# Moving searches, gathered rows and branch products between the stages of a transformer block on one Trainium2 core

## The chip, the core and the metric

The kernel runs on one core of one Trainium2 chip. The metric is the device time of one execution in microseconds; shown are the median of three runs and one further execution that was profiled. A core has five engines that work beside each other and wait for each other by semaphores: TensorE (PE in the profile, with its weight loads as PEld), VectorE (DVE), ScalarE (ACT), GpSimd (POOL) and SyncE (SP, which here only issues transfers). Transfers are issued from SP, ACT and POOL. The matrix engine writes to eight banks (PSUM); everything else lies in the core's memory of 128 partitions.

## What is computed

One residual block over 512 frames and 16 meta tokens, width 2048, in float32:

```python
hn = rmsnorm(h, g_mix);  proj = hn @ w_in          # c_q, c_kv, k_rope, q/k/v_sb, gate_a, gate_b
y_a = mla_attention(...)                           # 8 heads, softmax, chunk-causal
y_b = stick_breaking_attention(...)                # 8 heads
h = h + (sig(gate_a) * (y_a @ w_branch_a) + sig(gate_b) * (y_b @ w_branch_b)) @ w_out
xn = rmsnorm(h, g_ffn)                             # PEER: 8 heads, 16384 experts
s = einsum('thcd,hcnd->thcn', xn @ w_q, sub_keys)  # 2 x 128 scores for each head
s1, i1 = top_k(s[:, :, 0], 16); s2, i2 = top_k(s[:, :, 1], 16)
idx, g = best 16 of the 16 x 16 sums, softmax      # "routing"
h = h + sum_k g_k * gelu(u[idx_k] . xn) * v[idx_k]
out = rmsnorm(h, g_final)                          # meta tokens dropped
```

A product in full float32 is made of three products of rounded parts: the helper `mm3` (lines 258 to 261) multiplies the low part of the weight with the high part of the data, high with low, and high with high.

## The kernel before

Everything is laid out transposed: the width lies on the partitions in 16 pieces of 128, the tokens along the free dimension. The stages follow each other in one long Python function, `body`, that unrolls all loops.

**Weights.** Each weight tile of 128 x 1024 goes the same way (`wtile`, lines 232 to 253): SP loads it into a raw tile `wr` (four of them in rotation, `raw_half`, line 230), ACT rounds it into `wh` (L245), DVE, or POOL for some, subtracts to get `wl` (L246). A raw tile is free again when the subtraction has read it. `wh` and `wl` have three tiles each; two more lie in the tail of `hgh`/`hgl` during the expert loop, and one more in a pool of its own in the output stage.

**Mixer.** Projections, stick-breaking attention and gates, then MLA head by head: in each round of `run(...)` the scores of head h+1 (`mla_s`), the projections of head h+2 (`mla_p`) and the output of head h (`mla_y`) take turns. In the last head only `mla_y` is left. After that the stick-breaking output `yb` is split into high and low parts (eight splits, one for each head), and in the branch loop each of 16 blocks m needs one product with `wa` and one with `wb` (24 matrix products of 512 columns each), both multiplied by a gate. Then `w_out`.

**Scores.** For 16 blocks hc (head and half) PE computes the query block with `wq` in 48 products of 512 columns and the scores of the block before it for four token tiles (`scores`). DVE finds the sixteen highest of each score row by `top16`: MAX8, FIND_INDEX8, MATCH_REPLACE8, MAX8, FIND_INDEX8 (L917 to L921), for token tiles 3, 2, 0 and 1 in this order. The 184 last tokens (all of tile 3 and 56 of tile 2) take their experts' rows one by one: for each of 184 slots POOL gathers 128 rows of `u` by an indirect transfer (1 MB, `send`, L1052) and DVE multiplies and sums them (`row_step`, L1065), later the same with `v` (L1073). The routing of tile 3 (`early`) runs beside the score blocks, ten steps after every fourth block. From hc = 5 on each block ends with one row step.

**Expert loop.** For the other 328 tokens all 16384 experts are computed: e = 0 to 127, each e is two halves of 24 products of 328 columns (`u_products`). After each half `beside(hf)` gives DVE and PE other work: a step of the gates (`gating`: for each pair of tokens one DVE comparison L1256, four ACT scalings L1263, four small PE products L1252, and every 16 tokens a store to memory `g_d` from POOL), the row steps that are due (`rows_due`, with the due count interpolated in `PACE`), and steps of the routing of tiles 2, 0 and 1 (`routing`, a generator of `route` with 30 steps for each tile). Routing steps: one for each e below 8, two for each e from 8 to 23, from then on three for every two e. Gating of a tile starts when its routing is done. At e = 120 the first group's gates are read back (`group_in(0)`).

**Output stage.** 32 groups by 8 blocks of `vb`; each block is two column blocks c of 12 products of 328 columns, added into `acc` (L1498, L1500) unless the next group goes on in the same bank. The remaining 168 row steps are spread over these by `PACE_V`. At the end the squares of `acc` are summed over 16 column blocks (`fin_add`, L1420 and L1422), a product with ones gives the sum over partitions (`rstd`, L301), ACT and DVE form the inverse root (L309 to L315), DVE scales all 16 blocks (L1429), SP stores them (L1431). The last 184 columns go first (`fin_out(ND, SEQ)`), the other 328 at the very end (`fin_out(0, ND)`).

**Order.** The order of the instructions on each engine is fixed when the kernel is built, from the order of the text, the dependencies and an estimate of when things are ready; in the trace it is not simply the order of the text (the first product of the branch loop stands among the last head's products, at 964.09 us). `add_manual_dep(..., NOSYNC)` only keeps an instruction behind another in that order. Each engine then works strictly through its own list.

Of the kernel before, what the change touches and what calls it, by code (L numbers as in the profile page):

```python
# [2 lines left out]

# [20 lines left out]
P = 128  # L24
# [8 lines left out]
H = 8  # L33
# [182 lines left out]
def body(tc, nc, a, dbg=None):  # L216
# [12 lines left out]
    def raw_half():  # L229
        return wp.tile([P, 1024], F32, name="wr", tag="wr", bufs=4)  # L230
# [32 lines left out]
    def split(hi, lo, src, eng=None):  # L263
        S.activation(hi, src, AF.Copy)
        (eng or V).tensor_sub(lo, src, hi.bitcast(F32))
# [26 lines left out]
    xn_d = dp.tile([NB, D], F32, name="xn_d")  # L292
    xr_d = dp.tile([2, P, D], F32, name="xr_d")
# [532 lines left out]
    for m in range(KC):  # L826
        acc = []
        for name, yh_, yl_, gi in (("wa", *ys[0], 0), ("wb", *ys[1], 1)):
            gt = sp2.tile([P, SEQ], F32, name="g2", bufs=4)
            SP.dma_start(gt, gates[gi, m])  # L830
            wh, wl = front(name, m)
            ps = ps_tile()
            for k in range(8):
                s = slice(k * P, (k + 1) * P)
                mm3(ps, wh[:, s], wl[:, s], yh_[:, k], yl_[:, k], k == 0, k == 7)
# [187 lines left out]
    PACE = (0, 14, 60, NK - 0.5), (11, 28, 97, NU)  # L1023
# [7 lines left out]
    gs = {"sent": 0, "done": 0, "pool": None, "gated": False, "six": None, "third": False, "x": 1, "rows": None, "vi": None}  # L1031
# [65 lines left out]
    with tc.tile_pool(name="score", bufs=2, side="right") as sp_:  # L1097
# [8 lines left out]
        def scores(hc, qh, ql):  # L1106
# [8 lines left out]
            for ti in (3, 2, 0, 1):  # L1115
# [9 lines left out]
        for hc in range(16):  # L1125
            ps = ps_tile()
            for hf in range(2):
                wh, wl = wq.pop((hc, hf)) if (hc, hf) in wq else front("wq", hc, hf, G if hf else V)
                for k in range(8):
# [25 lines left out]
            split(qh, ql, ps)  # L1155
# [191 lines left out]
    for e in range(NK):  # L1347
# [67 lines left out]
    rf = ap2.tile([P, SEQ], F32, name="rf")  # L1415

    def fin_add(c, t0, t1, first):
        t = slice(t0, t1)
        sq = ssf if first else vp.tile([P, SEQ], F32, name="fsq", bufs=1)
        S.activation(sq[:, t], acc[:, c, t], AF.Square)  # L1420
        if not first:
            V.tensor_add(ssf[:, t], ssf[:, t], sq[:, t])  # L1422

    def fin_out(t0, t1):
        sc = vp.tile([P, D], F32, name="sc", tag="row", bufs=1).rearrange("p (k t) -> p k t", t=SEQ)
        rstd(rf[:, t0:t1], ssf[:, t0:t1], t1 - t0, D, [sc[:, k] for k in range(3)], None)
# [103 lines left out]
```

## Time and profile before

| | |
|---|---|
| median of 3 runs | 3457.99 us (3455.57 to 3458.05) |
| the profiled execution | 3459.31 us, of it the span of the core 3457.6 us |
| granted TensorE clock | 0.995 |
| PE, PEld busy | 99%, 92% of the span |
| DVE, ACT, POOL busy | 74%, 41%, 22% |
| moved by DMA | 919.94 MB, mean 266 GB/s |
| stages, us from the start of the span | mixer to about 965, branch and w_out to 1317, scores to 1519, expert loop to 2488, output stage to the end |

How to read it: a row of the busy-time view gives, for a stretch from A to B, its length and for each engine the busy time and in brackets the number of instructions, then the granted clock, the busy share of the DMA engines and GB/s. A row of the timeline gives start, duration, engine, line, operation, the tiles written and read, their shapes and a count; in square brackets the idle time before it and who ended it. PE's busy time counts overlapping, pipelined products, so that a stretch with PE busy throughout may still hold fewer products than another: the number in brackets is to be read with it.

### The profile page before, as it was taken

The page shows a single profiled execution, that of the slowest core. Times are in us where ns is not written, and L with a number is a line of the kernel's source. Part 1 is how long each engine was busy: PE and PEld are TensorE (multiplying, and loading weights), DVE is VectorE, ACT ScalarE, POOL GpSimd, SP SyncE. Part 2 cuts the span into 40 slices and gives each one's busy share as a digit, 9 for nine tenths or more (in the row PEclk, how much of TensorE's full clock was granted, in tenths as well). Part 3 has the DMA queues.
Part 4 walks back from the last instruction along what each step waited for, and adds up shares of the span by engine and source line. Part 5 has one row for each costly group of instructions (what it writes and reads, how often), then busy time and mean ns, then how long its engine had stood idle before and what let it go on. Part 6 is the DMA issues. An engine that isn't in the chain of part 4 may idle for free.

```text
span 3457.6 us, 53380 instructions
## 1 busy us (share of the span) xinstructions
PE 3420.5 (99%) x21115; PEld 3188.2 (92%) x21115; DVE 2573.5 (74%) x3573; ACT 1427.4 (41%) x2304; POOL 776.1 (22%) x555
## 2 busy tenths in 40 slices
PE   9999999999999999999999999999999999999997
PEld 8988888887888888889999999999999999999997
DVE  5533334445754557999999988887889999999997
ACT  4233333334543223223576776774333333333333
POOL 1000000000001113322333333333213333333320
PEclk9999999999999999999999999999999999999998
DMA  5322323232144345559999999999999999999993
GB/s 171 100 98 100 98 100 100 89 101 74 62 131 143 129 143 181 204 214 367 377 389 407 405 412 412 405 401 398 403 362 375 394 408 400 402 382 399 409 381 116
DMA packets 227141, 919.94 MB, mean 266 GB/s; under 512 B 27806, under 2 KB 53518, under 8 KB 179090
## 3 DMA queue, kind: packets, MB, share of 16 engines
q1 hardware_dynamic: 134660, 466.11, 36.6%
q0 software_dynamic: 60480, 411.68, 30.0%
q10 hardware_dynamic: 31750, 38.75, 3.1%
q8 instruction: 165, 2.70, 0.3%
q14 instruction: 86, 0.70, 0.1%
HBM read 854.57 MB, written 62.91 MB: 265 GB/s over the span
## 4 chain that ended last, share of the span: by engine, by line
PE 81%; DVE 11%; DMA 4%; issue 2%; ACT 1%; SPq 0%; POOL 0%; DVEq 0%; ACTq 0%
PE ps L259 26%; PE ps L260 25%; PE ps L261 25%; DMA wr<-vb 3%; DVE wl L246 3%; DVE xg L1073 1%; DVE row L1065 1%; PE ps L1252 1%; DVE acc L1073 1%; DVE acc L1500 1%; DVE hgl L246 0%; ACT wh L245 0%; DVE hin L1337 0%; DMA row<-u,eo 0%; DVE acc L1429 0%
## 5 line engine op out<-in xcount | busy, mean ns | idle before, releaser
L245 ACT ACTIVATE wh<-wr 128x1024 fp32r<-128x1024 f32 (+1 forms) x654 | 687.8, 1053 | 1402.6 <-PE ps L261 1038.7
L246 DVE TENSOR_TENSOR wl<-wr,wh 128x1024 fp32r<-128x1024 f32 (+1 forms) x639 | 812.0, 1279 | 391.5 <-ACT wh L245 389.3
L259 PE MATMUL ps<-vah,wl 128*128 128x328 f32 x2048 | 643.8, 314 | 7.0 <-DVE wl L246 6.8
L260 PE MATMUL ps<-val,wh 128*128 128x328 f32 x2048 | 642.7, 314 | 0.0
L261 PE MATMUL ps<-vah,wh 128*128 128x328 f32 x2048 | 639.7, 312 | 0.0
L259 PE MATMUL ps<-hgh,wl 128*128 128x328 f32 (+1 forms) x1488 | 490.9, 330 | 2.8 <-DVE wl L246 2.8
L261 PE MATMUL ps<-hgh,wh 128*128 128x328 f32 (+1 forms) x1488 | 486.1, 327 | 0.0
L260 PE MATMUL ps<-hgl,wh 128*128 128x328 f32 (+1 forms) x1488 | 485.8, 326 | 0.0
L259 PE MATMUL ps<-xh,wl 128*128 128x512 f32 (+1 forms) x1376 | 468.1, 340 | 1.5 <-ACT xh L366 1.5
L260 PE MATMUL ps<-xl,wh 128*128 128x512 f32 (+1 forms) x1376 | 465.0, 338 | 0.8 <-DVE xl L367 0.8
L261 PE MATMUL ps<-xh,wh 128*128 128x512 f32 (+1 forms) x1376 | 464.9, 338 | 0.0
L259 PEld LDWEIGHTS ps<-vah,wl 128*128 128x128 f32 x2048 | 386.3, 189 | 9.5 <-DVE wl L246 9.3
L260 PEld LDWEIGHTS ps<-val,wh 128*128 128x128 f32 x2048 | 387.1, 189 | 0.0
L261 PEld LDWEIGHTS ps<-vah,wh 128*128 128x128 f32 x2048 | 386.8, 189 | 0.0
L1052 POOL DMA_INDIRECT row<-v,eo x128 | 215.5, 1684 | 481.4 <-DVE xg L1073 414.4
L1073 DVE SCALAR_TENSOR_TENSOR xg<-row,act,xg 128x2048 f32<-128x2048 f32 x127 | 297.5, 2343 | 1.2 <-DMA row<-v,eo 1.1
L1065 DVE SCALAR_TENSOR_TENSOR row<-row,xg 128x2048 f32<-128x2048 f32 x128 | 292.1, 2282 | 4.8 <-DMA row<-u,eo 4.8
L259 PEld LDWEIGHTS ps<-hgh,wl 128*128 128x128 f32 x1488 | 280.1, 188 | 14.6 <-DVE wl L246 3.4
L261 PEld LDWEIGHTS ps<-hgh,wh 128*128 128x128 f32 x1488 | 280.1, 188 | 11.7 <-issue 0.2
L260 PEld LDWEIGHTS ps<-hgl,wh 128*128 128x128 f32 x1488 | 280.4, 188 | 10.9
L259 PEld LDWEIGHTS ps<-xh,wl 128*128 128x128 f32 x1376 | 258.6, 188 | 30.2 <-ACT xh L366 3.0
L260 PEld LDWEIGHTS ps<-xl,wh 128*128 128x128 f32 x1376 | 259.1, 188 | 29.1 <-DVE xl L367 1.7
(517 smaller groups left out, 6057.6 us busy)
## 6 DMA issues: line engine op xcount, KB each, us to landing
wr<-ut SPq DMA_DIRECT2D x256, 512.0 KB, 9.4
wr<-vb SPq DMA_DIRECT2D x256, 512.0 KB, 8.0
wr<-front SPq DMA_DIRECT2D x238, 512.0 KB, 3.3
g_d<-gb POOLq DMA_DIRECT2D x42, 512.0 KB, 10.9
gin<-g_d SPq DMA_DIRECT2D x32, 672.0 KB, 7.4
h_d<-hb ACTq DMA_DIRECT2D x128, 164.0 KB, 8.3
hin<-h_d SPq DMA_DIRECT2D x32, 656.0 KB, 8.9
gates<-gt ACTq DMA_DIRECT2D x32, 256.0 KB, 2.0
```

Of the source, the lines that this page charges most:

```text
L245: more["last"] = S.activation(hi[:, s], r, AF.Copy)
L246: sub = (eng or V).tensor_sub(lo[:, s], r, hi[:, s].bitcast(F32))
L259: T.matmul(ps, wl, xh, start=start, stop=False)
L260: T.matmul(ps, wh, xl, start=False, stop=False)
L261: T.matmul(ps, wh, xh, start=False, stop=stop)
L1052: G.indirect_dma_start(out=row, out_offset=None, in_=a[src], in_offset=bass.IndirectOffsetOnAxis(ap=eos[part][:, k:k + 1], axis=0))
L1065: ins = V.scalar_tensor_tensor(row, row, 1.0, xs[part], ALU.mult, ALU.mult, accum_out=w)
L1073: ins = V.scalar_tensor_tensor(y, row, w, y, ALU.mult, ALU.add)
L1252: T.matmul(bank[:, o:o + P], ohs[q % 4][:, 1, :, t], wos[:, q % 4, c, :, t], start=c == 1, stop=c == 0)
L1500: mark = V.tensor_add(acc[:, c, :ND], acc[:, c, :ND], ps[:, :ND])
```

## The change

There are seven edits.

1. **Fifth raw weight tile in the output stage.** When the extra weight pool is open, every fifth raw tile comes from it.
2. **Branch products ahead.** In the last two heads of MLA a new generator splits all eight heads of `yb` into tiles that lie where the MLA inputs were, and computes the `wb` products of blocks 0, 1 and 2 into PSUM banks that stay held (`ready`). In the run of head 6 it may take nine steps, in the run of head 7 all the rest. The branch loop then takes these three from `ready`. The eight splits at the start of the branch stage stay, for blocks 3 to 15.
3. **One token tile's searches put off.** `scores` no longer searches tile 1; it stores its scores to memory (`s_d`, one store from the ACT queue for each block). After the routing of tile 0, four loads of four blocks each on the SP queue bring them back, into the tile that the candidates of the routing use, and 16 searches follow as routing steps.
4. **Rows earlier.** From hc = 11 a second row step stands in the middle of each score block, and `PACE` is (16, 38, 101, 200) in place of (11, 28, 97, 200) at e = 0, 14, 60 and 127.5.
5. **Routing steps.** They begin after e = 5 and come at an even rate of 1.5 for each e.
6. **Gating steps.** Every fourth e takes one more.
7. **Output.** The squares of the 328 columns get a second tile; the last column block's square isn't added on DVE, PE adds it in PSUM behind a product with the sum of the other fifteen; the inverse root takes fewer DVE instructions; the stores are in smaller groups.

The core of the diff:

```diff
     def raw_half():
+        if more["pool"] is not None and more["n"] % 5 == 0:
+            return more["pool"].tile([P, 1024], F32, name="wr", tag="wr")
         return wp.tile([P, 1024], F32, name="wr", tag="wr", bufs=4)
...
+    s_d = dp.tile([P, 2 * H, NK], F32, name="s_d")
...
+    AHEAD = 3
+    ready = {}
+    def branch_ahead():
+        bh, bl = ([lp.tile([P, 4, n], F32R, name=x, tag=t)[:, :, :SEQ] for t, n in ((f"cq{p}", SEQ), (f"ck{p}", LEN))]
+                  for x, p in (("ybh", "h"), ("ybl", "l")))
+        for h in range(H):
+            split(bh[h // 4][:, h % 4], bl[h // 4][:, h % 4], yb[:, h])
+            yield
+        for m in range(AHEAD):
+            wh, wl = front("wb", m)
+            ps = ready[m] = ps_tile()
+            for k in range(8):
+                s = slice(k * P, (k + 1) * P)
+                mm3(ps, wh[:, s], wl[:, s], bh[k // 4][:, k % 4], bl[k // 4][:, k % 4], k == 0, k == 7)
+                if k % 2:
+                    yield
...
+        if h == H - 2:
+            ahead = branch_ahead()
+        run(*([mla_s(h + 1)] if h + 1 < H else []), *([mla_p(h + 2)] if h + 2 < H else []), mla_y(h),
+            *([ahead] if h == H - 1 else [islice(ahead, 9)] if h == H - 2 else []))
...
+            if gi and m in ready:
+                ps = ready.pop(m)
+            else:
...
-    PACE = (0, 14, 60, NK - 0.5), (11, 28, 97, NU)
+    PACE = (0, 14, 60, NK - 0.5), (16, 38, 101, NU)
...
-            for ti in (3, 2, 0, 1):
+            S.dma_start(s_d[:, hc], sc[:, 1])
+            for ti in (3, 2, 0):
...
+                if hf and hc > 10:
+                    row_step(more["dve"], 2)
...
             yield from route(ti, 4, rk)
             routed.append(ti)
+            for h0 in range(0, 2 * H if ti == 0 else 0, 4):
+                sc = rk.tile([P, 512], F32, name="sc4", tag="cand", bufs=1).rearrange("p (h n) -> p h n", n=NK)
+                ld = SP.dma_start(sc, s_d[:, h0:h0 + 4])
+                tc.add_manual_dep(ld.ins, more["last"].ins.name, NOSYNC, reason="not before its turn")
+                for _ in range(3):
+                    yield
+                for h in range(4):
+                    top16(v1[:, 1, h0 + h], i1[:, 1, h0 + h], sc[:, h], NK)
+                    yield
...
-            next(gate_steps, None)
+            for _ in range(2 if hf and e % 4 == 0 else 1):
+                next(gate_steps, None)
...
-            for _ in range(hf if e < 8 else 1 if e < 24 or e % 2 else hf):
+            while gs["steps"] < 1.5 * (e + hf / 2 - 5):
+                gs["steps"] += 1
...
+    def fin_last(c):
+        ps = final["ps"] = ps_tile()
+        T.matmul(ps[:, :ND], ones, ssf[:, :ND], start=True, stop=False)
+        sq = vp.tile([P, ND], F32, name="fsq", bufs=2)
+        S.activation(sq, acc[:, c, :ND], AF.Square)
+        T.matmul(ps[:, :ND], ones, sq, start=False, stop=True)
+
+    def fin_end():
...
+        S.activation(t, ps, AF.Ln, scale=1.0 / D, bias=C("eps"))
+        V.tensor_scalar(v, ps, 1.0 / D, EPS, ALU.mult, ALU.add)
+        S.activation(r0, t, AF.Exp, scale=-0.5)
+        V.tensor_mul(v, v, r0)
+        V.scalar_tensor_tensor(v, v, -0.5, r0, ALU.mult, ALU.mult)
+        V.scalar_tensor_tensor(rf, v, 1.5, r0, ALU.add, ALU.mult)
+        for c0, n in ((0, 1), (1, 1), (2, 2), (4, 2), (6, 2), (8, 2), (10, 2), (12, 2), (14, 1), (15, 1)):
```

More of the change, by code (lines that the diff above doesn't have):

```diff
@@ L2 @@
 from contextlib import ExitStack
+from itertools import islice
 import numpy as np
@@ L264, in split @@
         S.activation(hi, src, AF.Copy)
-        (eng or V).tensor_sub(lo, src, hi.bitcast(F32))
+        return (eng or V).tensor_sub(lo, src, hi.bitcast(F32))
     def dump(name, ap):
@@ L830, in body @@
             SP.dma_start(gt, gates[gi, m])
[L831 to L835, printed above, removed]
+            if gi and m in ready:
+                ps = ready.pop(m)
+            else:
+                wh, wl = front(name, m)
+                ps = ps_tile()
+                for k in range(8):
+                    s = slice(k * P, (k + 1) * P)
+                    mm3(ps, wh[:, s], wl[:, s], yh_[:, k], yl_[:, k], k == 0, k == 7)
             sg = S.activation(gt, gt, AF.Sigmoid)
@@ L1030, in body @@
     rcols = [rcol] + [rcolb[:, j:j + 1] for j in range(len(cuts))]
-    gs = {"sent": 0, "done": 0, "pool": None, "gated": False, "six": None, "third": False, "x": 1, "rows": None, "vi": None}
+    gs = {"sent": 0, "done": 0, "pool": None, "gated": False, "six": None, "third": False, "x": 1, "steps": 0, "rows": None, "vi": None}
     rows = {}
@@ L1154, in body @@
                 S.dma_start(xn_d, xgb[:NB])
-            split(qh, ql, ps)
+            more["dve"] = split(qh, ql, ps)
             late.append((hc, qh, ql))
@@ L1414, in body @@
     ssf = ap2.tile([P, SEQ], F32, name="ssf")
-    rf = ap2.tile([P, SEQ], F32, name="rf")
     def fin_add(c, t0, t1, first):
         t = slice(t0, t1)
-        sq = ssf if first else vp.tile([P, SEQ], F32, name="fsq", bufs=1)
-        S.activation(sq[:, t], acc[:, c, t], AF.Square)
+        sq = ssf[:, t] if first else vp.tile([P, ND], F32, name="fsq", bufs=2)[:, :t1 - t0]
+        S.activation(sq, acc[:, c, t], AF.Square)
         if not first:
-            V.tensor_add(ssf[:, t], ssf[:, t], sq[:, t])
+            V.tensor_add(ssf[:, t], ssf[:, t], sq)
     def fin_out(t0, t1):
         sc = vp.tile([P, D], F32, name="sc", tag="row", bufs=1).rearrange("p (k t) -> p k t", t=SEQ)
+        rf = sc[:, 3]
         rstd(rf[:, t0:t1], ssf[:, t0:t1], t1 - t0, D, [sc[:, k] for k in range(3)], None)
@@ L1431, in fin_out @@
             SP.dma_start(a["out"][c0:c0 + n, :, t0:t1].rearrange("k p t -> p k t"), acc[:, c0:c0 + n, t0:t1])
+    final = {}
+    def fin_last(c):
[5 more added lines that the diff above has]
+    def fin_end():
+        sc = vp.tile([P, D], F32, name="sc", tag="row", bufs=1).rearrange("p (k t) -> p k t", t=SEQ)
+        v, r0, t, rf = (sc[:, k, :ND] for k in range(4))
+        ps = final["ps"][:, :ND]
+        S.activation(t, ps, AF.Ln, scale=1.0 / D, bias=C("eps"))
[5 more added lines that the diff above has]
+        for c0, n in ((0, 1), (1, 1), (2, 2), (4, 2), (6, 2), (8, 2), (10, 2), (12, 2), (14, 1), (15, 1)):
+            for c in range(c0, c0 + n):
+                V.scalar_tensor_tensor(acc[:, c, :ND], acc[:, c, :ND], gain("fin")[:, c:c + 1],
+                                       rf, ALU.mult, ALU.mult)
+            SP.dma_start(a["out"][c0:c0 + n, :, :ND].rearrange("k p t -> p k t"), acc[:, c0:c0 + n, :ND])
     banks_of, begun, done = {}, {STAY[0] * 2 + c for c in range(4)}, []
@@ L1504, in body @@
                 if i >= NG - 1 and not stays:
-                    fin_add(c, 0, ND, not done)
+                    if len(done) == KC - 1:
+                        fin_last(c)
+                    else:
+                        fin_add(c, 0, ND, not done)
                     done.append(c)
@@ L1509, in body @@
     assert sorted(done) == list(range(KC))
-    fin_out(0, ND)
+    fin_end()
     fin.close()
```

1 line of the change is left out of this document (removed).

## The prediction

> **What bounds the kernel now.** I read the page first, then who makes PE wait, then the busy times of short stretches to find where PE stands still.
>
> ```profile
> span 3457.6 us, 53380 instructions
> PE 3420.5 (99%) x21115; PEld 3188.2 (92%) x21115; DVE 2573.5 (74%) x3573; ACT 1427.4 (41%) x2304; POOL 776.1 (22%) x555
> PE ps L259 <- DVE wl L246: 9.6, 8, 2.4
> ```
>
> PE is the bound: it idles 37.1 us in all, and the change takes no product away. So only idle PE can be won, and what follows an idle PE. Eight waits for DVE's subtraction (9.6 us) are the only large ones. The stretches (from:to, length, then busy time and instructions of PE, PEld, DVE, ACT, POOL, granted clock, DMA share, GB/s) show where:
>
> ```profile
> 950.00:965.00 15.00, 12.88 (x80) 10.11 (x79) 11.02 (x34) 8.08 (x23) 0.00 (x0) 1.00 0.00 1
> 975.00:980.00 5.00, 5.00 (x24) 4.14 (x23) 3.43 (x3) 1.69 (x2) 1.28 (x1) 1.00 0.49 155
> 1415.00:1540.00 125.00, 124.58 (x646) 106.65 (x646) 122.49 (x454) 32.63 (x42) 29.90 (x19) 1.00 0.56 193
> 1540.00:1545.00 5.00, 2.63 (x16) 2.37 (x15) 5.00 (x25) 2.81 (x4) 2.25 (x2) 0.92 0.41 103
> 1545.00:1550.00 5.00, 5.00 (x27) 5.00 (x27) 4.71 (x8) 1.71 (x3) 0.94 (x1) 0.74 0.96 376
> 1550.00:1582.00 32.00, 32.00 (x215) 31.59 (x214) 31.89 (x79) 14.06 (x17) 8.05 (x6) 1.00 0.97 379
> 1820.00:1825.00 5.00, 3.85 (x26) 3.59 (x25) 2.81 (x6) 1.06 (x1) 0.98 (x1) 1.00 1.02 378
> 2505.00:2510.00 5.00, 4.50 (x30) 4.23 (x29) 5.00 (x5) 1.06 (x1) 1.68 (x1) 1.00 0.97 350
> 2525.00:2530.00 5.00, 3.65 (x24) 3.38 (x23) 5.00 (x5) 2.12 (x2) 1.49 (x2) 1.00 1.01 369
> 2530.00:2535.00 5.00, 4.56 (x20) 4.56 (x21) 5.00 (x6) 0.00 (x0) 0.94 (x1) 0.66 0.96 368
> 2555.00:2560.00 5.00, 3.66 (x24) 3.26 (x23) 5.00 (x5) 1.18 (x2) 2.61 (x2) 1.00 0.78 275
> 2560.00:2565.00 5.00, 3.21 (x21) 2.95 (x20) 5.00 (x6) 1.06 (x1) 0.94 (x1) 0.98 1.04 418
> 2565.00:2570.00 5.00, 5.00 (x25) 5.00 (x25) 5.00 (x5) 0.00 (x0) 0.94 (x1) 0.68 0.98 404
> 2575.00:2580.00 5.00, 5.00 (x36) 5.00 (x35) 2.84 (x4) 2.20 (x3) 0.00 (x0) 1.00 1.01 410
> 2580.00:3380.00 800.00, 798.91 (x5323) 797.90 (x5323) 750.87 (x636) 267.59 (x248) 261.37 (x150) 1.00 0.99 391
> ```
>
> The reader should see five places. At the end of the mixer (950 to 965) PE idles 2.12 us. At the start of the expert loop (1540) it idles 2.37 us, and then the granted clock falls to 0.74 and 27 products fit where an undisturbed 5 us hold 36: 9 x 0.14 = 1.3 us more. At 1820 it idles 1.15 us. In the first 80 us of the output stage the idle times are 0.50 + 1.35 + 0.44 + 1.34 + 1.79 = 5.4 us, and the slow clock after them costs 12 products in 2530 to 2535 (20, where 4.56 us hold 32) and 11 in 2565 to 2570, 23 x 0.14 = 3.2 us: 8.6 us. Afterwards (2580 to 3380) 1.1 us in 800. The last place is the tail, below.
>
> **The end: minus 1.0 us.** After the last product of the output stage a chain runs alone (DVE but for the second row).
>
> ```profile
> 3441.20 0.50 DVE L1422 TENSOR_TENSOR ssf<-ssf,fsq 128x328 f32<-128x328 f32 x1 [0.60 <-ACT fsq L1420]
> 3441.76 1.22 PE L301 MATMUL ps<-ssf,cst 128*128 128x328 f32 x2 [2.32 <-DVE ssf L1422]
> 3443.57 0.50 DVE L310 TENSOR_SCALAR sc<-ps 128x328 f32<-128x328 f32 x1 [1.88 <-ACT sc L309]
> 3444.08 0.50 DVE L312 TENSOR_TENSOR sc<-sc 128x328 f32<-128x328 f32 x1
> 3445.52 0.50 DVE L315 TENSOR_TENSOR rf<-sc 128x328 f32<-128x328 f32 x1
> 3446.05 7.62 DVE L1429 SCALAR_TENSOR_TENSOR acc<-acc,gn,rf 128x328 f32<-128x328 f32 x16
> ```
>
> The addition at 3441.20 goes (0.50), as PE starts on the square itself. From 3444.08 to 3446.05 four instructions make the root, 1.97 us; three of 0.50 make 1.5, another 0.47 saved. The new product with the sum of fifteen blocks is ready one block earlier and hidden by the last addition and square; uncovered it costs half of 1.22. The 16 scalings stay, and the stores behind them keep their last two pieces, so smaller groups in front I take at nothing (between 0 and -1). Together -1.0, from -2 to -0.3.
>
> **Branch products ahead: minus 2 us.** 72 products at 5 us for 24 make 15 us of work that waits for nothing but the splits, beside an idle time of 2.12 us. The price is on DVE and ACT, where the eight splits are made a second time:
>
> ```profile
> 966.22 4.90 DVE L265 TENSOR_TENSOR yl_b<-yb,yh_b 128x512 fp32r<-128x512 f32 x8
> ```
>
> 4.9 us more on DVE, which is busy 11.0 of the 15 us: 15.9 in 15. That delays the last head's output by about 1 us, but PE has the 15 us of products to do meanwhile. The three weights come earlier on SP, ACT and DVE and are not loaded twice. The second set of splits gets its memory only when the products ahead are done; `wa` of blocks 0 to 3 (four times 5 us) covers these 5 us. Three of eight banks are held, none is lacking. If PE reaches the first product before the splits, the 4.9 us show: -2.1 to +5. I take -2, as the work at hand is seven times the hole.
>
> **Score blocks and start of the expert loop: plus 3 us.** DVE decides: it is busy 122.5 of 125 us from 1415, and 31.9 of 32 after the hole. Prices:
>
> ```profile
> L1065 DVE SCALAR_TENSOR_TENSOR row<-row,xg 128x2048 f32<-128x2048 f32 x128 | 292.1, 2282 | 4.8 <-DMA row<-u,eo 4.8
> L919 DVE MATCH_REPLACE8 wk<-lists,sc 128x128 f32<-128x128 f32 x64 | 17.5, 274 | 0.0
> L921 DVE FIND_INDEX8 lists<-lists,wk 128x8 uint32<-128x128 f32 x64 | 18.1, 283 | 0.0
> L987 DVE TENSOR_TENSOR oh<-oh,step 128x1024 f16<-128x1024 f16 x2 | 1.4, 688 | 0.0
> 1572.78 1.19 DVE L246 TENSOR_TENSOR wl<-wr,wh 128x1024 fp32r<-128x1024 f32 x1
> 1574.18 0.31 PE L259 MATMUL ps<-hgh,wl 128*128 128x328 f32 x1
> L1052 POOL DMA_INDIRECT row<-u,eo x128 | 169.2, 1322 | 468.5 <-DVE row L1065 284.0 <-DVE lists L917 45.2 <-DVE tv L920 35.6
> ```
>
> A row step is 2.28 us, a search five instructions of 0.27 to 0.28, 1.4 us. The pair of DVE and PE shows how little is in hand near e = 8 (by the count of products it begins near 1582): the weight is ready at 1573.97, the product that needs it starts at 1574.18. So the sum goes from 1415, where DVE has no more slack (block 8), to e = 8. Rows: `PACE` and the five extra steps make 29 instead of 21, 8 x 2.28 = +18.2. Searches: nine blocks lose one, 9 x 1.4 = -12.6. Routing: by the step counts four or five of tile 2's steps instead of eight; those not yet due are the unpacking and two one-hot builds of 0.69, some -2.7. Sum +2.9 us, and each of them moves PE, since DVE is full on both sides. Bounds: if the first score blocks from 8 on now leave DVE idle, the searches of three are saved for nothing: +7. If the hole at 1540 closes, because routing has not begun there, and the overload finds routing steps to put off: -3.7. I take +3.
>
> Gathers move with the rows: two in a block of 12.6 us (1317 to 1519 for 16); POOL is busy 29.9 of 125 us there and takes 1.3 us for one; queued behind it is its own weight subtraction. The 16 stores of `sc` stand in ACT's queue; ACT is busy 32.6 of 125. Nothing for both.
>
> **Later routing: minus 1.15 us.** After e = 14 the rows come at 63 for 46 e instead of 69, so DVE gets slack where it was full, and the 16 searches (22 us) fall between e = 48 and 64. The hole at 1820, one late DVE subtraction, should be covered. The four loads on SP wait for the candidate tile; weight loads stand behind them and the cast of the weights waits for those. In cover is about one half (3.6 us); uncovered +2 for each of four. By counted steps gating ends at e = 116.5 instead of 110.5. The first group's gates are read at e = 120; 3.5 x 7.1 us (48 products at 215 in 32 us) = 25 us are enough for a store of
>
> ```profile
> g_d<-gb POOLq DMA_DIRECT2D x42, 512.0 KB, 10.9
> ```
>
> **Fifth raw tile: minus 6 us.** What leads to the holes at 2525 (DVE, ACT):
>
> ```profile
> 2503.20 2.35 DVE L1073 SCALAR_TENSOR_TENSOR acc<-row,actb,acc 128x2048 f32<-128x2048 f32 x1
> 2505.47 4.62 DVE L246 TENSOR_TENSOR wl<-wr,wh 128x1024 fp32r<-128x1024 f32 x4
> 2512.10 1.49 DVE L1337 TENSOR_TENSOR hin<-hin,gin 128x1280 f32<-128x1280 f32 x1 [2.01 <-issue]
> 2517.05 1.22 DVE L246 TENSOR_TENSOR wl<-wr,wh 128x1024 fp32r<-128x1024 f32 x1 [3.36 <-ACT wh L245]
> 2515.96 1.06 ACT L245 ACTIVATE wh<-wr 128x1024 fp32r<-128x1024 f32 x1 [8.62 <-DMA wr<-vb]
> wr<-vb SPq DMA_DIRECT2D x256, 512.0 KB, 8.0
> ACT wh L245 <- DMA wr<-vb: 200.0, 62, 10.2
> ```
>
> DVE is behind, does four subtractions in a row, frees four raw tiles at once; the loads take 8 us, ACT waits 8.6, DVE stands idle 5.4 us, and then has rows and weights at once and makes PE wait at 2525. The same again at 2555. One more raw tile is loaded during the burst, so that one subtraction (1.2 us) falls into DVE's idle time. Each of the two groups (about 2 us and the slow clock, then 3.1 us and the slow clock) loses at least 1.2, probably with it the fall of the clock. Of 8.6 us I take two thirds, -6. Bounds: -9.5 with the waits after 2580; +7 below.
>
> **Sum:** -1.0 - 2.0 + 3 - 1.15 - 6 = -7.15 us. Profiled execution: 3459.31, of it 1.7 outside the span, so 3452.2; the median shown lies 1.3 lower, at 3457.99: forecast 3450.8 us. About 0.2%, 6.9 us, is what a measurement of this kernel can tell from no change; the forecast is just beyond.
>
> **Rivals.** (1) All holes close: -2 at the end, -2.1, -3.7, -1.15, -8.6: 3440.4. For it: every edit aims at a place where PE idles, and DVE's load later falls. Against: eight more rows in a stretch where DVE is full. (2) The holes of the output stage only move, since rows, not loads, put DVE behind (a row of 2.35 us stands right ahead of the four subtractions): the V term is 0 and the time 3456.8; the change then does not do there what it says. (3) The start of the expert loop takes it: +7 and a second fall of the clock, 1.3, in place of +3: 3456.1. (4) Slower: the fifth load joins the burst. DMA is at 0.99 from 2580 on and at 0.97 to 1.04 in most rows of the holes; five loads of 512 KB take 5/4 of the 8.6 us, 2.2 us more at each of three bursts, which a DVE that is busy 750.9 of 800 us does not make up: +6.5, and two falls of the clock more, 3: 3466. It decides once a burst frees all five. [...]
>
> **How the numbers follow.** Forecast 0.45 (own range 3446 to 3455), (1) 0.22, (2) 0.15, (3) 0.08, (4) 0.10. Faster by over 0.2% (below 3451.1): half of the forecast and (1), 0.45; slower (above 3464.9): most of (4), 0.08; else 0.47. The range leaves out (4) and the lower third of (1): 3440 to 3461.
>
> **What would show it.** Right: in 950 to 965 PE busy throughout; a chain end of 1 us less; in the first 80 us of the output stage at most half of the idle time and one or no fall of the clock; leads near zero and a hole of 2 to 6 us between e = 0 and 14; PE full around e = 40. Wrong: a hole at the splits; ACT waiting longer for `wr<-vb` than 200 us in all; no hole in the expert loop, then rows cost less than reckoned.

## The result and the profile after

The changed kernel takes 3477.04 us (median of 6 runs, 3469.95 to 3480.45); the kernel before took 3457.24 us in the 6 runs beside it (3454.25 to 3462.2). The ratio is 1.0058, with a 95% interval from 1.0046 to 1.0070: slower by about 20 us, where 7 us of gain were forecast. The profiled execution took 3478.51 us, its span is 3476.7 us. Of the medians below one leaves out an execution: a_turn_four_rows_back once took 5570.83 us at a granted clock of 0.562.

First the page of the kernel after, then three rows of its waits (who waited and for whom: us in total, times, longest):

```profile
span 3476.7 us, 53463 instructions
...
PE 3430.7 (99%) x21117; PEld 3197.5 (92%) x21117; DVE 2578.0 (74%) x3579; ACT 1422.1 (41%) x2312; POOL 755.8 (22%) x555
```
```profile
ACT wh L248 <- DMA wr<-vb: 31.6, 11, 8.3
...
DVE lists L945 <- DMA sc<-s_d: 18.3, 2, 9.2
...
PE ps L262 <- DVE wl L249: 13.4, 7, 4.5
```

PE stands 46.0 us where it stood 37.1, and is "busy" 10.2 us longer with practically the same products (two records more), mainly in slow clock: before the last 40 us the clock records of the trace stand at half speed for 47.8 us in all, those of the kernel before for 20.5. The second row is new: twice DVE stood still, 18.3 us in all, for the scores that come back from memory. The busy times of short stretches of the kernel after (columns as in the prediction) show the same places as before, and as new ones one in the last score block (1500) and two around 1870 and 1950:

```profile
945.00:965.00 20.00, 19.16 (x110) 15.03 (x110) 16.23 (x48) 10.80 (x31) 0.00 (x0) 1.00 0.14 47
1500.00:1505.00 5.00, 3.80 (x23) 3.21 (x22) 5.00 (x18) 0.00 (x0) 1.27 (x1) 1.00 0.47 187
1505.00:1510.00 5.00, 5.00 (x16) 3.95 (x15) 4.93 (x9) 2.33 (x4) 0.95 (x1) 0.66 0.71 230
1545.00:1550.00 5.00, 1.71 (x9) 1.72 (x10) 5.00 (x10) 3.01 (x4) 0.99 (x1) 0.93 0.94 347
1550.00:1555.00 5.00, 5.00 (x26) 5.00 (x26) 5.00 (x13) 0.07 (x1) 1.08 (x2) 0.72 0.98 392
1820.00:1825.00 5.00, 5.00 (x40) 4.89 (x39) 5.00 (x7) 3.65 (x10) 1.72 (x1) 1.00 1.04 353
1865.00:1870.00 5.00, 3.21 (x22) 2.94 (x20) 1.51 (x10) 1.62 (x3) 0.00 (x0) 1.00 0.48 194
1870.00:1875.00 5.00, 2.51 (x9) 2.51 (x10) 5.00 (x16) 0.83 (x1) 0.09 (x1) 0.52 0.39 136
1945.00:1950.00 5.00, 3.85 (x29) 3.58 (x25) 1.03 (x8) 0.00 (x0) 0.00 (x0) 1.00 0.87 353
1950.00:1955.00 5.00, 1.11 (x4) 1.11 (x5) 4.97 (x21) 0.80 (x3) 0.00 (x0) 0.71 0.08 12
2515.00:2520.00 5.00, 1.25 (x9) 0.98 (x7) 0.53 (x1) 1.62 (x2) 0.00 (x0) 0.87 0.60 248
2520.00:2525.00 5.00, 4.25 (x15) 4.25 (x16) 5.00 (x5) 1.33 (x2) 0.94 (x1) 0.50 0.35 107
2530.00:2535.00 5.00, 2.54 (x11) 2.27 (x10) 5.00 (x5) 1.06 (x1) 3.28 (x2) 0.74 0.92 319
```

At the end of the mixer 0.84 us of idle PE are left of 2.12. The start of the expert loop is worse (1500, 1545). The hole at 1820 is closed. But at 1865 to 1875 and 1945 to 1955 PE stands 4.3 and 5.0 us and then runs slowly, and in the first row of each DVE is busy for only 1.51 and 1.03 us of 5: no engine is overloaded there, something is being waited for. The holes at the start of the output stage have changed their place, but they are not gone.

**A ledger of stages.** The trace holds every product `ps<-..,wl` or `ps<-..,hgl` of the expert loop (2048, sixteen for each e) and of the output stage (2048, 64 for each group), so number 16e starts block e, and the difference of two such starts is exactly what a stage took. Lengths of the stages in the profiled executions, in us, all so worked out (the columns add up to the span but for rounding):

| kernel | to scores | scores to e = 8 | e 8 to 44 | e 44 to 64 | e 64 to output | groups 0 to 3 | rest | span |
|---|---|---|---|---|---|---|---|---|
| before | 1317.2 | 264.4 | 272.3 | 153.8 | 480.3 | 125.0 | 844.5 | 3457.6 |
| after | 1314.6 | 268.6 | 267.0 | 169.5 | 485.5 | 126.3 | 845.1 | 3476.7 |
| a_no_loads | 1316.5 | 268.9 | 270.6 | 157.6 | 482.5 | 123.9 | 842.9 | 3463.0 |
| a_in_turn | 1314.7 | 268.4 | 266.8 | 154.4 | 485.5 | 127.8 | 838.0 | 3455.5 |
| a_act_loads | 1314.2 | 267.6 | 267.0 | 161.6 | 485.0 | 128.9 | 841.1 | 3465.5 |
| a_four_in_scores | 1316.7 | 279.1 | 270.6 | 152.9 | 483.2 | 122.6 | 842.5 | 3467.6 |
| a_turn_four | 1314.2 | 268.5 | 270.8 | 152.8 | 482.7 | 124.1 | 843.5 | 3456.5 |
| a_turn_four_rows_back | 1316.5 | 259.1 | 269.2 | 155.0 | 488.7 | 121.9 | 847.7 | 3458.1 |
| a_turn_late | 1316.7 | 267.2 | 266.6 | 155.3 | 487.5 | 117.8 | 838.0 | 3449.0 |
| best_mid | 1314.6 | 262.0 | 273.6 | 153.1 | 486.5 | 119.4 | 841.0 | 3450.3 |
| b_ahead_out | 1315.2 | 264.3 | 272.5 | 154.9 | 480.3 | 121.5 | 845.1 | 3453.8 |
| b_ahead_out_fifth | 1315.1 | 264.4 | 273.4 | 153.9 | 480.3 | 126.8 | 843.2 | 3457.0 |
| b_fifth_late | 1316.1 | 264.2 | 272.1 | 153.9 | 480.3 | 119.0 | 843.8 | 3449.3 |
| best_two_rows | 1314.7 | 265.0 | 270.9 | 156.0 | 480.6 | 118.4 | 841.6 | 3447.4 |

So the 19.1 us between the two spans are -2.6 + 4.2 - 5.3 + 15.7 + 5.2 + 1.3 + 0.6. Most of it lies between e = 44 and 64. For example, the rows from which that column comes, of the kernel before and of the kernel after:

```profile
1853.91 0.31 PE L259 MATMUL ps<-hgh,wl 128*128 128x328 f32 x1
...
2007.76 0.32 PE L259 MATMUL ps<-hgh,wl 128*128 128x328 f32 x1
```
```profile
1850.22 0.40 PE L262 MATMUL ps<-hgh,wl 128*128 128x328 f32 x1
...
2019.73 0.32 PE L262 MATMUL ps<-hgh,wl 128*128 128x328 f32 x1
```

One profiled execution of each kernel stands behind a row; stages without any edit between two kernels differ by up to some 2 us (the first column of those with branch products ahead goes from 1314.2 to 1316.7), and up to some 7 us in the last one, where clock falls come and go (before the last 40 us the clock stands at half speed for 6.8 us of it in the kernel before, for 17.1 in the kernel after). The profiled execution of a_in_turn is the fastest of its ten (3457.28 us). The medians further down are therefore read beside the ledger; those of runs made at different times have kernels before of 3456.86 to 3459.04 us beside them, so that a difference between two of them is better taken from their ratios.

**What happens at 1856.** From the timelines of SP, ACT, DVE and PE of the kernel after, in this order:

```profile
1856.00 0.42 SPq L1327 DMA_DIRECT2D sc<-s_d  x1
...
1861.91 1.06 ACT L248 ACTIVATE wh<-wr 128x1024 fp32r<-128x1024 f32 x1 [2.67 <-DMA wr<-ut]
...
1865.71 1.06 ACT L248 ACTIVATE hgh<-wr 128x1024 fp32r<-128x1024 f32 x1 [2.74 <-DMA wr<-ut]
...
1858.25 1.16 DVE L249 TENSOR_TENSOR hgl<-wr,hgh 128x1024 fp32r<-128x1024 f32 x1
...
1868.49 0.49 DVE L945 MAX8 lists<-sc 128x8 f32<-128x128 f32 x2 [9.08 <-DMA sc<-s_d]
...
1871.22 1.21 DVE L249 TENSOR_TENSOR wl<-wr,wh 128x1024 fp32r<-128x1024 f32 x1
...
1872.49 0.64 PE L262 MATMUL ps<-hgh,wl 128*128 128x328 f32 x1 [4.28 <-DVE wl L249]
```

The load of four blocks' scores is issued at 1856.00. DVE has finished its last subtraction at 1859.41, and next in its fixed order stands the first search. It waits 9.08 us, until 12.5 us after the issue. Meanwhile ACT has rounded two weights (1862.97, 1866.77) whose subtractions stand behind the search. The first of them is done at 1872.43, and PE, out of weights, starts at 1872.49. The third of the four does the same (SP, DVE, PE):

```profile
1936.07 0.43 SPq L1327 DMA_DIRECT2D sc<-s_d  x1
...
1948.97 0.29 DVE L945 MAX8 lists<-sc 128x8 f32<-128x128 f32 x1 [9.23 <-DMA sc<-s_d]
...
1953.89 0.64 PE L262 MATMUL ps<-hgh,hgl 128*128 128x328 f32 x1 [5.04 <-DVE hgl L249]
```

The change keeps the load behind a weight's rounding and lets three routing steps pass in the text; but nothing kept the searches behind those steps, so they moved up in DVE's order to right behind the load.

### The profile page after: what moved, and what is told of

The parts are those of the page before. It is cut to its first block, busy times and chain, and to the rows that moved or that the text cites. A ratio compares the mean times of both kernels' runs of the same rounds, so it can differ in the third digit from the quotient of the medians.

```text
span 3476.7 us, 53463 instructions
## 1 busy us (share of the span) xinstructions
PE 3430.7 (99%) x21117; PEld 3197.5 (92%) x21117; DVE 2578.0 (74%) x3579; ACT 1422.1 (41%) x2312; POOL 755.8 (22%) x555
## 4 chain that ended last, share of the span: by engine, by line
PE 70%; DVE 13%; DMA 9%; issue 4%; ACT 2%; POOL 1%; SPq 0%; DVEq 0%; ACTq 0%; POOLq 0%
PE ps L262 22%; PE ps L263 22%; PE ps L264 22%; DMA wr<-ut 6%; DVE row L1093 4%; DVE wl L249 2%; DVE hgl L249 1%; DMA sc<-s_d 1%; ACT wos L1294 1%; POOL row L1080 1%; ACT wh L248 1%; DMA wr<-vb 1%; DMA g_d<-gb 0%; DVE more_oh L1287 0%; DMA row<-u,eob 0%
## 5 line engine op out<-in xcount | busy, mean ns | idle before, releaser
L1080 POOL DMA_INDIRECT row<-v,eo x128 | 203.0, 1586 | 481.3 <-DVE xg L1101 430.2
```

The source lines that it names most:

```text
L1080: G.indirect_dma_start(out=row, out_offset=None, in_=a[src], in_offset=bass.IndirectOffsetOnAxis(ap=eos[part][:, k:k + 1], axis=0))
```

## Experiments

Theory A is the paragraph above: DVE stands in order in front of the data. Rivals for the loss between e = 44 and 64 were B (weight loads are late, queued on SP behind the four loads: the prediction's own view) and C (22 us of searches are too much). For the output stage they were D (the holes only move), E (the prediction: the fifth raw tile gains) and F (one load more in flight lengthens the others); G (the first load into the fifth tile comes late) was added from the order of the loads on SP. H says that DVE is full at the start of the expert loop, so that rows placed there move PE. The measured medians (ratios to the kernel before on the same chip, with 95% intervals) stand with each.

**a_no_loads** leaves out the four loads, so that the searches read zeros and the output is not the block's; **a_in_turn** changes the order alone:

```diff
 # a_no_loads
-                ld = SP.dma_start(sc, s_d[:, h0:h0 + 4])
-                tc.add_manual_dep(ld.ins, more["last"].ins.name, NOSYNC, ...)
+                V.memset(sc, 0.0)
 # a_in_turn
-                    top16(v1[:, 1, h0 + h], i1[:, 1, h0 + h], sc[:, h], NK)
+                    first = top16(v1[:, 1, h0 + h], i1[:, 1, h0 + h], sc[:, h], NK)   # its first MAX8
+                    tc.add_manual_dep(first.ins, more["lo"].ins.name, NOSYNC, reason="not before its data")
```

> The changed kernel (3477.0 us) without its four loads of the put-off scores: the 16 searches run at the same steps, over a tile of zeros written by DVE, so the searched values are left out. Its trace has 16.8 us of standing and slowly clocked TensorE between e = 44 and 64. Theory A (the data come late: DVE stands in its fixed order in front of the first search of a loaded four, 9.1 and 9.2 us, with weight subtractions behind it): these go, 3461 to 3464. Rival B (SP: the weight loads queued behind the four loads arrive late): the same 3461 to 3464. Rival C (22 us of searches are too much for DVE in this stretch): 3474 to 3480.

> The changed kernel with all four loads, but the first search of each block is kept behind the last weight subtraction of its step in DVE's order, so that DVE reaches it about two e (15 us) after the load was issued, where the trace has 12.4 us from issue to landing. Theory A (DVE stands before the data): the holes between e = 44 and 64 shrink from 16.8 to under 4 us, 3462 to 3466. Rivals B (weight loads late behind the loads on SP) and C (too many searches): holes of 12 us or more remain, 3473 to 3479.

Measured: 3464.32 us (1.0019, 1.0009 to 1.0029) and 3463.54 us (1.0014, 1.0005 to 1.0024); the stage from e = 44 to 64 took 157.6 and 154.4 us, where the kernel after took 169.5 and the kernel before 153.8. a_in_turn has all four loads on SP and all 16 searches, so B and C fall and A is shown: some 13.5 us of the 20 (15 by the ratios and by the stage) are an order of instructions on DVE. The same place in a_in_turn (SP, then DVE):

```profile
1855.82 0.43 SPq L1328 DMA_DIRECT2D sc<-s_d  x1
...
1859.15 1.21 DVE L249 TENSOR_TENSOR wl<-wr,wh 128x1024 fp32r<-128x1024 f32 x1
...
1872.63 1.23 DVE L249 TENSOR_TENSOR wl<-wr,wh 128x1024 fp32r<-128x1024 f32 x1 [4.77 <-ACT wh L248]
...
1875.98 0.29 DVE L945 MAX8 lists<-sc 128x8 f32<-128x128 f32 x1
```

The load is issued at the same time and the search starts 20 us later, without waiting, after four subtractions and three rows that had stood behind it (the first and the last of the subtractions are shown; two lie between them). a_no_loads says less than was meant: with nothing to wait for, its searches do not stay at their steps but run between 1801.6 and 1878.5 us, twelve of the sixteen before e = 44 (1856.06), where the kernel after has them between 1868.5 and 1999.6. So it is no test of C, and why it keeps 3 us more than a_in_turn in this stage is open.

**a_act_loads**: the four loads from another queue.

```diff
-                ld = SP.dma_start(sc, s_d[:, h0:h0 + 4])
+                ld = S.dma_start(sc, s_d[:, h0:h0 + 4])
```

> The changed kernel (3477.0 us) with its four loads issued from ACT's queue in place of SP's. Theory A1 (the data take 12.5 us since all transfers share the same engines, whose share is near 1 there): landing in 8 to 13 us, DVE still stands, 3473 to 3479. Rival A2 (they wait behind the weight loads in SP's queue): landing in 2 to 5 us, half of the holes gone, 3465 to 3471.

Measured: 3469.3 us (1.0038, 1.0025 to 1.0051), outside A1's range and in A2's. The time from issue to use is A1's all the same. ACT's issues and DVE's first searches in its timeline:

```profile
1853.04 0.45 ACTq L1327 DMA_DIRECT2D sc<-s_d  x1
...
1931.92 0.33 ACTq L1327 DMA_DIRECT2D sc<-s_d  x1
```
```profile
1865.03 0.49 DVE L945 MAX8 lists<-sc 128x8 f32<-128x128 f32 x2 [7.61 <-DMA sc<-s_d]
...
1940.79 0.49 DVE L945 MAX8 lists<-sc 128x8 f32<-128x128 f32 x2 [4.21 <-DMA sc<-s_d]
```

From issue to use it took 12.0 and 8.9 us from ACT's queue, 12.5 and 12.9 from SP's: A1's 8 to 13 us hold, and SP's queue is not where most of that time goes. Whether the 4 us of the second load are SP's queue or the traffic of the moment these two pairs don't tell. DVE waits 11.8 us in place of 18.3, because the later of the two came 4 us sooner and because ACT issued each about 1 us earlier against DVE's own place (DVE began to wait 4.4 and 4.7 us after the issue, before 3.4 and 3.7). So the loss shrank with the wait, by 7.9 us of the 16 between e = 44 and 64. That all transfers share the same engines, A1's reason, no run tested. The busy share of the DMA engines was about 1 in the middle of DVE's first wait, in the kernel after (0.89 over the whole of it) and in a_act_loads:

```profile
1860.00:1865.00 5.00, 5.00 (x36) 5.00 (x35) 0.00 (x0) 1.06 (x1) 0.22 (x1) 1.00 1.03 418
```
```profile
1860.00:1865.00 5.00, 5.00 (x36) 5.00 (x35) 0.00 (x0) 1.69 (x2) 0.00 (x0) 1.00 1.01 410
```

**b_ahead_out** and **b_ahead_out_fifth**: the kernel before with edits 2 and 7, and with edit 1 as well.

```diff
 # only in b_ahead_out_fifth
     def raw_half():
+        if more["pool"] is not None and more["n"] % 5 == 0:
+            return more["pool"].tile([P, 1024], F32, name="wr", tag="wr")
```

> The kernel before with two of the seven edits only: branch products ahead, and the output edit. In the trace after, the products stand 2.6 us earlier at the start of the score blocks and the stretch from the last addition into acc to the end is 1.6 us shorter. Theory (both are independent of the rest): 3457.2 - 4.2 = 3453.0, from 3452 to 3454.5. Rival (the gain of the first is eaten in the score blocks, where DVE is full): 3455 to 3457.

> As b_ahead_out with the fifth raw tile in the output stage as well. Theory D (rows and transfers, not the number of raw tiles, put DVE behind at the start of the output stage; the holes only move, as they did in the trace after, where the first three groups lost 1.1 us more than before): within 2 us of b_ahead_out, 3451 to 3455. Rival E (the prediction's term: the fifth tile takes two thirds of the 8.6 us; what the trace after shows there comes from the other edits): 6 us under b_ahead_out, about 3447. Rival F (the fifth load joins the burst): 3 to 9 us over it.

Measured: 3452.64 us (0.9981, 0.9971 to 0.9990), as the theory said, and 3455.5 us (0.9988, 0.9979 to 0.9997), so the fifth tile cost 2.9 us where the prediction had it gain 6. That excludes E; between D and F, and from no cost at all, the medians don't decide, as the two intervals overlap. Groups 0 to 3 take 126.8 us with it, 121.5 without. The order in which SP issues the loads of the output stage, by the names that the tiles have in the built program (23476 is the stage's first weight, 23586 its fourth; `select` is a small load that stands between), is in b_ahead_out and in b_ahead_out_fifth:

```
b_ahead_out:        23476 23515 23552 23586 23623 23666 23698 select 23733
b_ahead_out_fifth:  23476 23515 23552 23623 23666 23698 23733 select 23586
```

The fourth weight is the first that takes the fifth raw tile. The memory of the new tile is in use until the end of the expert loop, so its load waits for PE, and has moved behind four later weights. SP, ACT and PE of b_ahead_out_fifth:

```profile
2488.63 0.40 SPq L246 DMA_DIRECT2D wr<-vb  x1
...
2500.36 2.95 ACT L248 ACTIVATE wh<-wr 128x1024 fp32r<-128x1024 f32 x3 [8.50 <-DMA wr<-vb]
...
2502.72 0.64 PE L262 MATMUL ps<-vah,wl 128*128 128x328 f32 x1 [4.74 <-DVE wl L249]
```

The load goes out at 2488.63, two weights after it are there already when it lands (three roundings follow each other at 2500.36), and PE has waited 4.74 us for it. This is theory G.

**b_fifth_late** makes the test: the same fifth tile, used from the third five on.

```diff
         if more["pool"] is not None and more["n"] % 5 == 0:
-            return more["pool"].tile([P, 1024], F32, name="wr", tag="wr")
+            more["fives"] = more.get("fives", 0) + 1
+        if more.get("fives", 0) > 2 and more["n"] % 5 == 0:
+            return more["pool"].tile([P, 1024], F32, name="wr", tag="wr")
```

> As b_ahead_out_fifth (3455.5 us), but the fifth raw tile is used from the third five of weights on, no longer for the fourth weight of the output stage. In the order on SP of b_ahead_out_fifth that fourth weight's load stands four places later than in b_ahead_out (3452.6 us), waits there for the last product of the expert loop, whose memory it takes, and lands at 2500.36, where TensorE has stood since 2497. Theory G (that one late first load is the loss): the holes of 4.9 and 2.2 us at 2497 and 2512 go, 3447 to 3452.5. Rival F (one more load in flight lengthens the others): 3454 to 3458.

Measured: 3447.25 us (0.9972, 0.9962 to 0.9982), the lowest median of all kernels here: 5.4 us under b_ahead_out and 8.3 under b_ahead_out_fifth, by the ratios 3.1 and 5.5. The ledger's column for groups 0 to 3 says it more clearly, over all kernels: the five with four raw tiles take 121.5 to 125.0 us (mean 123.0), the five with the fifth tile as the change has it 123.9 to 128.9 (126.7), the four with it late 117.8 to 119.4 (118.7). G is shown, F falls: in b_fifth_late the first load into the fifth tile stands behind `select` and waits for PE just so (it goes out at 2486.69), but it carries the fourteenth weight, which is needed only later. The stretches at 2500 and 2525 and those where b_ahead_out lost 2.3 us (2555 to 2565), in b_fifth_late:

```profile
2500.00:2505.00 5.00, 4.73 (x32) 4.46 (x30) 5.00 (x4) 1.30 (x2) 2.71 (x2) 1.00 0.93 337
2525.00:2530.00 5.00, 3.21 (x22) 2.94 (x21) 5.00 (x6) 1.06 (x1) 0.94 (x1) 1.00 1.01 393
2530.00:2535.00 5.00, 5.00 (x34) 4.79 (x33) 5.00 (x5) 1.06 (x1) 0.94 (x1) 1.00 0.99 404
2555.00:2560.00 5.00, 5.00 (x36) 5.00 (x35) 5.00 (x5) 2.12 (x2) 0.29 (x2) 1.00 1.02 420
2560.00:2565.00 5.00, 5.00 (x35) 5.00 (x34) 5.00 (x5) 1.06 (x1) 1.73 (x2) 1.00 1.03 415
```

One hole of 1.79 us is left, and 0.27 us at 2500; the group around 2560 is closed, as the prediction had argued for a tile that is loaded in the burst.

**a_turn_late** puts both repairs (a_in_turn and b_fifth_late) into the changed kernel.

> The changed kernel with both repairs: searches kept in their turn, and the fifth raw tile from the third five on. Theories A and G together: a_in_turn (3463.5 us) less the 8 us by which b_fifth_late (3447.3) is under b_ahead_out_fifth (3455.5): 3454 to 3457; what then remains against b_fifth_late, 7 to 9 us, is edits 3 to 6. Rival (the start of the output stage is late for another reason here): 3459 to 3463.

Measured: 3451.62 us (0.9988, 0.9979 to 0.9997), 25.4 us under the changed kernel (24.2 by the ratios) and lower than expected. The two flaws explain the whole loss; with them mended the change is faster than the kernel before, only just clear of no change, though 4.4 us slower than its edits 1, 2 and 7 alone, so edits 3 to 6 together bring nothing.

**Rows and searches at the start of the expert loop.** a_turn_four is a_in_turn without edit 1; a_turn_four_rows_back takes edit 4 out of it; a_four_in_scores takes edit 3 out of the changed kernel, again with four raw tiles.

```diff
 # a_turn_four_rows_back, against a_turn_four
-                if hf and hc > 10:
-                    row_step(more["dve"], 2)
-    PACE = (0, 14, 60, NK - 0.5), (16, 38, 101, NU)
+    PACE = (0, 14, 60, NK - 0.5), (11, 28, 97, NU)
 # a_four_in_scores, against the changed kernel (edit 1 undone as well)
-            S.dma_start(s_d[:, hc], sc[:, 1])
-            for ti in (3, 2, 0):
+            for ti in (3, 2, 0, 1):
```

> a_in_turn (3463.5 us) without the fifth raw tile. By the fifth tile's price between b_ahead_out and b_ahead_out_fifth (2.9 us) and by theory G: 3459 to 3461.5, and the first four groups of the output stage lose about 9 us instead of 15. Rival (the gates end so late that the start of the output stage is short of transfers in any case): 3463 to 3465.

> a_turn_four with the rows at the old pace (no second row step in the score blocks, 11, 28, 97 at e = 0, 14, 60). Theory H (eight more rows until e = 8 make the holes there: 1.35 us in the last score block and 7.6 us of holes and slow clock from e = 0 to 8 in a_in_turn): these shrink by 4 to 8 us, and the stretch from e = 8 to 44 gives 1 to 3 back: 3454 to 3458. Rival (the holes come from the unpacking of the routing and the weights that meet there, not from rows): no change against a_turn_four, 3459 to 3462.

> The changed kernel with four raw tiles and without the putting off: token tile 1 is searched in the score blocks again (no stores, no loads), the rows stay early. Theory H (DVE is full from block 8 on, and what is added there moves TensorE): from the start of the score blocks to e = 8 it takes 10 to 20 us more than a_turn_four, and the holes between e = 44 and 64 are gone: 3466 to 3478. Rival (DVE has room in the score blocks): 3458 to 3462.

Measured: 3460.72 us (1.0011, 1.0002 to 1.0020), 3459.01 us (1.0006, 0.9997 to 1.0015) and 3470.24 us (1.0040, 1.0026 to 1.0054). In the ledger the rows cost 268.5 - 259.1 = 9.4 us between the score blocks and e = 8, about half of their 18 us of DVE, and the 16 searches, put back there, cost 279.1 - 268.5 = 10.6 of their 22 us. So H holds for the place: what DVE gets there moves PE, by about half of its price. It fails for the time: without the early rows the stage from e = 44 to 64 takes 2.2 us more, that from 64 to the output 6.0, the last one 4.2 (within that column's scatter), and the medians are the same within the intervals. The stretches where the kernel after had its holes, in a_turn_four_rows_back:

```profile
1500.00:1505.00 5.00, 5.00 (x30) 4.27 (x29) 4.90 (x24) 2.51 (x4) 3.25 (x2) 1.00 0.55 175
1545.00:1550.00 5.00, 5.00 (x36) 5.00 (x35) 5.00 (x13) 2.45 (x3) 1.51 (x2) 1.00 1.00 398
```

The hole at 1545 holds theory A's mechanism once more, in small. ACT, DVE and PE of the kernel after:

```profile
1532.42 1.06 ACT L248 ACTIVATE hgh<-wr 128x1024 fp32r<-128x1024 f32 x1 [3.77 <-DMA wr<-ut]
...
1544.18 2.29 DVE L1093 SCALAR_TENSOR_TENSOR row<-row,xg 128x2048 f32<-128x2048 f32 x1 [2.43 <-issue]
...
1547.02 1.22 DVE L249 TENSOR_TENSOR hgl<-wr,hgh 128x1024 fp32r<-128x1024 f32 x1
...
1548.29 0.42 PE L262 MATMUL ps<-hgh,hgl 128*128 128x328 f32 x1 [3.38 <-DVE hgl L249]
```

The weight was rounded at 1533.48 and its subtraction came 13.5 us later; DVE was full until 1541.75 and then stood 2.43 us in front of a row. The view calls this "issue", but the landings in the trace tell what it waited for: the row's gather, which POOL issued at 1536.61 and which landed at 1544.10, 0.08 us before the row began. a_turn_four has such an idle time there too, of 2.21 us (landed 1543.35, row from 1543.43), and a_turn_four_rows_back, where the gather landed at 1541.06 and the row came at 1541.63, has none.

**best_mid** and **best_two_rows** look for a place where these rows come free: (11, 18, 56, 101) rows at e = 0, 5, 28, 60 in a_turn_late without the extra row steps, and (11, 15, 26, 97) at e = 0, 6, 14, 60 in b_fifth_late.

> a_turn_late without the extra row steps in the score blocks and with 11, 18, 56, 101 rows at e = 0, 5, 28, 60: no more rows than the kernel before until e = 5, more of them from e = 5 to 28, where a_turn_four_rows_back lost only 1.05 us in 20 e, and fewer after. Theory H (rows cost where DVE has no slack, and come free between e = 5 and 28): no hole at e = 3, and none of the 3.35 us between e = 28 and 44 and the 6.9 us between 84 and 108: 3441 to 3447. Rival (any place for these rows makes holes of the same sum): 3449 to 3455.

> b_fifth_late (3447.3 us) with some two to three rows fewer until e = 6: 11, 15, 26, 97 rows at e = 0, 6, 14, 60 in place of 11, 28, 97 at 0, 14, 60. Its trace stands 2.58 us at e = 3 and has some 1.3 us of slow clock behind it, while DVE is full. Theory H (rows set how late DVE is there; two rows are 4.6 us of DVE): that hole closes and none opens before e = 44, 3442 to 3445. Rival (the rows put off make holes of the same sum later, as best_mid's and a_turn_four_rows_back's did between e = 28 and 44): 3446 to 3450.

Measured: 3451.92 us (0.9986, 0.9977 to 0.9994) and 3451.26 us (0.9979, 0.9971 to 0.9988): the rivals' numbers or worse. best_mid won 5.2 us up to e = 8 against a_turn_late and gave 7.0 back from e = 8 to 44; in best_two_rows the hole at e = 3 only went to e = 5. In these two kernels, rows moved by a few e took their hole with them.

## Why the prediction was wrong

The forecast sum was -7.15 us, and the profiled spans differ by +19.1. Of these 26 us between the two, 17 lie in the stages of the later routing (e = 8 to the output) and 7 in groups 0 to 3, where the fifth raw tile was to gain; the stages of the other three terms lie within 1.6 us of theirs. No rival had a time above 3466 us, and none had DVE standing in front of data. Point by point, by the prediction's own terms (profiled executions, forecast against what the ledger gives):

- **The end, -1.0.** Right in mechanism, too small. From the last addition into `acc` to the start of the last scalings the kernel before took 3446.05 - 3440.11 = 5.94 us, the kernel after 4.75, and the stores behind took 0.44 less: -1.6. The row of the kernel before and two of the kernel after (the other row stands in the prediction):

```profile
3440.11 0.49 DVE L1500 TENSOR_TENSOR acc<-acc,ps 128x328 f32<-128x328 f32 x1
```
```profile
3460.84 0.50 DVE L1567 TENSOR_TENSOR acc<-acc,ps 128x328 f32<-128x328 f32 x1 [0.19 <-PE ps L264]
...
3465.59 7.62 DVE L1496 SCALAR_TENSOR_TENSOR acc<-acc,gn,sc 128x328 f32<-128x328 f32 x16
```

- **Branch products ahead, -2.** Right within the scatter of that column: -2.6 here, -0.5 to -3.0 in the other kernels that have them (1316.7 to 1314.2 against 1317.2). No hole at the splits.
- **Score blocks and start of the expert loop, +3.** Right in mechanism and place: +4.2, a hole of 1.2 us in the last block with DVE busy throughout, and one of 3.4 at e = 3. That DVE itself stood 2.4 us in front of a row's gather ahead of it was not foreseen. That the sum came so near is in part luck: the rows were priced at 18.2 us and the searches at -12.6, each moving PE in full, but the rows cost 9.4 where the searches are gone (a_turn_four against a_turn_four_rows_back) and the searches 10.6 where the rows are there (a_four_in_scores against a_turn_four). Both prices were too high, with opposite signs, and what one costs depends on the other.
- **Later routing, -1.15.** This is the step of the prediction that failed. The hole at 1820 did close, but the four loads were priced as a wait on SP ("weight loads stand behind them", +2 for each if uncovered, taken at nothing). Their price lay on the other side, with the reader: DVE in front of the data, 9.1 and 9.2 us, its weight subtractions behind it. The stage from e = 44 to 64 took 15.7 us more, of which a_in_turn takes back 15.1. The prediction named who is queued behind the wait on SP, but did not ask the same for the engine that uses the data. The 5.2 us after e = 64 stand against 5.3 won from e = 8 to 44. Some of the latter is probably only moved, since the gates, which end 6 e later as counted, take their PE time later; no run separates that.
- **The fifth raw tile, -6.** This step failed as well. For the tile as the prediction imagined it the mechanism holds and the size is somewhat high (4.4 us in groups 0 to 3 by the means over all kernels, 3.1 to 5.4 between b_ahead_out and b_fifth_late). For the tile as it is the term is wrong: "one more raw tile is loaded during the burst" fails for the first load, which waits for memory that only comes free behind the expert loop, and PE waits for that weight (4.74 us in b_ahead_out_fifth). The view that would have said so was not in a profile but in the code: the pool is opened after the loop's pools are closed. The prediction's sign for "wrong", more than 200 us of ACT waiting for `wr<-vb`, did not show: that wait fell from 200.0 to 31.6 us, and groups 0 to 3 took 1.3 us longer. So ACT's waiting is no measure of what bounds this stage: it is 21.6 us in b_ahead_out_fifth and 23.6 in b_fifth_late.

Of the rivals, (2) came nearest for the output stage (the holes moved), though not for its reason: b_fifth_late shows that raw tiles, not rows, were short. (3) was 2.8 us short of its price (+4.2 of +7). (4), the only slower one, named the wrong mechanism: with the same fifth load in flight b_fifth_late is the fastest, at a DMA share of 0.93 to 1.03 in the rows shown.

## What to carry to other kernels

When data take a detour through memory, price the wait of the engine that uses them: ask what stands behind the first use in its order, give the load its measured time from issue to landing (here 12.5 us), and tie the use, not only the load, to a later place. When a buffer is added, ask what its memory held before, and let its first use come after that is free. A full engine need not give back the time that it is spared in one place: here rows moved by a few blocks took their holes with them, while products put into an idle time, a shorter chain at the end and transfers that came in time moved the end.

## What the hardware showed

The clock falls after some short holes and not after others of the same length. In the kernel after, 1.20 us of idle PE (1500 to 1505) were followed by a granted clock of 0.66 over 5 us and 16 products; in b_fifth_late 1.79 us (2525 to 2530) by none, 34 products at 1.00 in the next 5 us. In the kernel before a hole of the same 1.79 us (2528.65 to 2530.44) was followed by 0.66. Behind both falls the trace has a clock record of 3.41 us at 0.5 (from 1504.96 and from 2530.69), which gives the 0.66 over 5 us (0.5 x 3.41 + 1.59 = 3.3 of 5).

In the clock records of these two traces the falls between 900 and 3400 us begin whole multiples of 3.41 us apart (in the kernel after at 1504.96, 1549.34, 1870.19, 1952.11, 2518.72, 2532.38, 2651.84 and 3092.16, in the kernel before at 1544.23, 2530.69, 2564.82, 3073.40 and 3394.26), go to 0.5 and last 3.41 or 6.83 us. Counted in steps of 3.41 us from these times, the hole of 1.79 us in the kernel before lies inside one step (2527.27 to 2530.69); one of 1.34 us there (2557.54 to 2558.88) is cut by a border into 0.45 and 0.88 us, and the step behind it stayed at 1.00. Of the steps not already slow, all eight with 1.79 us or more of idle PE were followed by a fall, one of the three with 1.1 to 1.75 us (the one of 1.20 above; those of 1.15 and 1.41 in the kernel before were not), and none of the six with 0.5 to 1.1. Another four falls stand behind steps without any idle time; the one at 2651.84 in the kernel after follows 22 products of only 8 columns each. What sets off a fall, and why none followed the 1.79 us in b_fifth_late, is not shown; no run was made to test it.

So in these two traces 1.79 us of idle time within one step were enough each time, and 1.20 us once. What a fall adds to a hole is an estimate from the length and depth of the records: up to 1.7 us (half of 3.41) for each slow step, of which two follow the holes of 4.28 and 5.04 us in the kernel after.
